# Three of seven products by 512-column passes in a fused encoder layer on one Trainium2 core

## The chip, the cores and the metric

The kernel runs on one core of one Trainium2 chip. The metric is the device time of one execution in microseconds. Engines are named as in the profile: PE (TensorE), with its weight loads PEld apart, DVE (VectorE), ACT (ScalarE), POOL (GpSimd) and SP (SyncE), which issues most of the transfers.

## The reference

One encoder layer on x of 512 positions by 1024 channels, all in float32: a half-step SwiGLU, a mixer (a Fourier group beside grouped-query attention), and a second half-step SwiGLU, each behind an RMSNorm, with a last RMSNorm at the end. The change lies in the two SwiGLUs alone; their inner width is 2752.

```python
def swiglu(h, w_gate, w_up, w_down):
    return (jax.nn.silu(h @ w_gate) * (h @ w_up)) @ w_down

x = x + 0.5 * swiglu(rms_norm(x, ffn1_norm), ffn1_w_gate, ffn1_w_up, ffn1_w_down)
...
x = x + 0.5 * swiglu(rms_norm(x, ffn2_norm), ffn2_w_gate, ffn2_w_up, ffn2_w_down)
return rms_norm(x, final_norm)
```

## The kernel before

Activations lie turned, channels on the partitions and the 512 positions along the row. Every float32 operand is held as a high part, rounded to float32r, and a low part, the rest; a product is three: high by high, high by low, low by high.

**The FFN.** The inner width is cut into 21 blocks of 128 columns (j = 0 to 20) and a tail "t". `ffn` runs once for each SwiGLU. The first four blocks (three in the second FFN) and the tail go through plain gate and up products (`gate`, tile gu). All later ones, 17 and 18, go through `seven`: gate and up of a block together are a two-by-two matrix product over halves of the channels and halves of the positions, made in seven half-sized products in place of eight. The blocks form four groups; behind each stand its down products (`down`, tile dn), which go on while the next block's weights are prepared.

**The seven products.** For a block j, `prepare` loads gate and up weights (raw_g, raw_u), makes four sums (s1 to s4, in tiles s12 and s34) and splits seven weight operands into high and low parts in slots of 1024 words of the tile ring: a11 and a12 together, s1 and s2 together, s3 and s4 together (`both`: high parts in one slot, low parts in another), and a22 alone (`single`: its high part in a slot's first 512 words and its low part in the last). The seven operands on the activation side, b11, b22, b21 and t1 to t4, are made once per FFN by `operands`, in four steps i of one channel tile each, and lie in the tile rt: 2048 words each, high and low parts side by side in 256 + 256 columns, the n-th beginning at n * 2048 + PART_AT[n].

`multiply` runs one product in KH = 4 k steps. For weights not named in WIDE a step has three passes of 256 columns: high weights by high operand and by low operand into the same 256 columns (L436), and low weights by high operand (L441). For those in WIDE the first two are one pass of 512 columns over the operand's high and low parts (L432), which leaves two half sums in 512 columns of PSUM, and the low weights' pass goes to the first 256; both read and write in a turned order of four-word pieces. Whoever takes the result then adds the halves (`added`, `kept`). `step` gives the order on PE per block: a11 (into bank r), a12 (bank p), a22 of the block before (into that block's r), s1 (bank q), s2 (r), s4 (q), s3 (r). PIECES says behind which of them which part of the next block's preparation is recorded.

**Orders.** In the FFNs the order of PE and SP is the order in which the code records; DVE, ACT and POOL are ordered by a scheduler. `lows` is a subtraction on DVE. `rest_by_dma` makes a low part in another way: ACT writes the negated high part (L159), and a transfer issued by POOL adds the source onto it (L160). In `single` the low part of a22 comes from `lows`; in `operands` the b parts of the later steps i come from `rest_by_dma`, the t parts from `lows`. In the opening of an FFN some gates' weights take `rest_by_dma` too (gates 5 to 7 of the first FFN, gate 3 of the second).

Of the kernel before, what the change touches and what calls it, by code (L numbers as in the profile page):

```python
# [7 lines left out]
F32R = mybir.dt.float32r  # L8
# [5 lines left out]
P = 128  # L14
S = 512
# [11 lines left out]
ROOM = 64  # L27
# [5 lines left out]
GROUPS2 = ((0, "t", 1), range(2, 8), range(8, 14), range(14, 21))  # L33
PLACES = 7
HALF = S // 2
PART_AT = (0, 48, 96, 128, 128, 128, 128)
WIDE = ('a12', 's4')
USES = "a11", "a12", "s1", "s2", "s4", "s3", "a22"
PIECES = (0, 2, 2, 0, 2, 1, 1)
KH = KD // 2  # L40
# [43 lines left out]
def asf(ap):  # L84
    return ap.bitcast(F32)
# [3 lines left out]
def encoder(ctx, tc, A, out):  # L89
# [39 lines left out]
    def lows(lo, src, hi):  # L129
        nc.vector.tensor_tensor(out=lo, in0=src, in1=asf(hi), op=ALU.subtract)  # L130
# [26 lines left out]
    def rest_by_dma(lo, hi, src):  # L157

        nc.scalar.activation(lo, asf(hi), AF.Copy, scale=-1.0)  # L159
        nc.gpsimd.dma_start(out=lo, in_=src, accum_op=ALU.add)  # L160
# [18 lines left out]
    def turned(ap):  # L179
        return ap.rearrange("p (a b c) -> p b a c", b=4, c=4)  # L180
# [103 lines left out]
    def ffn(norm, after, wgu, wd, wdt, groups, opening, closing):  # L284
# [4 lines left out]
        n_ = norm.n  # L289
        n_plain = len(groups[0])  # L290
        with tc.tile_pool(name=f"act{n_}", bufs=1) as ap, tc.tile_pool(name=f"sums{n_}", bufs=2) as sp:
            room(ap, 128)
            acts = ap.tile([P, PLACES * 2 * S + ROOM], F32R, name=f"at{n_}")
            at = acts[:, FRONT + LOWER : FRONT + LOWER + PLACES * 2 * S].rearrange("p (n a b) -> p n a b", a=2, b=S)
            rt = ap.tile([P, 7 * KH * S + PART_AT[-1] + PART_AT[-1] - PART_AT[-2]], F32R, name=f"rt{n_}")
            wt, raws = [], {}
            free, where = list(range(PLACES)), {}

# [33 lines left out]

            begins = [i * KH * S + o for i, o in enumerate(PART_AT)]
            part = {
# [4 lines left out]
            def parts_at(i0, i1, i):  # L339

                step = begins[i0 + 1] - begins[i0] if i1 > i0 + 1 else KH * S
                c = rt[:, begins[i0] : begins[i0] + (i1 - i0) * step].rearrange("p (n r) -> p n r", r=step)
                return (c[:, :, i * S + o * HALF : i * S + (o + 1) * HALF] for o in range(2))

            def operands(rp, i0, i1):
                for i in range(i0, i1):
                    b = sp.tile([P, 4, HALF], F32, tag="raw_g", name=f"b{n_}_{i}")
                    for o, k in ((0, i), (2, i + KH)):
                        nc.vector.scalar_tensor_tensor(
                            out=b[:, o : o + 2].rearrange("p a b -> p (a b)"), in0=x[k],  # L350
                            scalar=gains[:, norm.n, k : k + 1], in1=rp, op0=ALU.mult, op1=ALU.mult,
                        )
                    b12, b11, b22, b21 = (b[:, o] for o in range(4))
                    t = sp.tile([P, 4, HALF], F32, tag=("s12", "s34")[i % 2], bufs=1, name=f"t{n_}_{i}")
                    for o, (p, q) in enumerate(((b12, b11), (b22, t[:, 0]), (b22, b12), (b21, t[:, 1]))):
                        nc.vector.tensor_tensor(out=t[:, o], in0=p, in1=q, op=ALU.subtract)
                    for src, i0, i1 in (b[:, 1:], 0, 3), (t, 3, 7):
                        h, l = parts_at(i0, i1, i)
                        nc.scalar.copy(h, src)
                        if i0 or i < (1 if n_ else 2):  # L360
                            lows(l, src, h)
                        else:
                            rest_by_dma(l, h, src)
# [4 lines left out]
            def take():  # L368

                taken.append((own or shared).pop(0))  # L370
                return taken[-1]
# [6 lines left out]
            def prepare(j):  # L378

                g = sp.tile([P, KD * P], F32, tag="raw_g", name=f"raw_g{n_}_{j}")  # L380
                u = wp.tile([P, KD * P], F32, tag="raw", name=f"raw_u{n_}_{j}")
                for t, c in ((g, 2 * j), (u, 2 * j + 1)):
                    nc.sync.dma_start(out=t.rearrange("p (a b) -> p a b", b=P), in_=wgu[c])
                a11, a12, a21, a22 = g[:, :S], g[:, S:], u[:, :S], u[:, S:]
                s12 = sp.tile([P, 2 * S], F32, tag="s12", bufs=1, name=f"s12_{n_}_{j}")
                s34 = sp.tile([P, 2 * S], F32, tag="s34", bufs=1, name=f"s34_{n_}_{j}")
                w = {}

                def both(names, src):
                    hi, lo = (take() for _ in range(2))  # L390
                    nc.scalar.copy(hi, src)  # L391
                    lows(lo, src, hi)
                    for i, n in enumerate(names):
                        w[n] = tuple(t[:, i * S : (i + 1) * S] for t in (hi, lo))
                    w[max(names, key=USES.index), "slots"] = hi, lo

                def single(n, src):
                    t = take()
                    hi, lo = t[:, :S], t[:, S:]
                    nc.scalar.copy(hi, src)  # L400
                    lows(lo, src, hi)
                    w[n] = hi, lo
                    w[n, "slots"] = (t,)

                def combine(out, a, b, op):
                    nc.vector.tensor_tensor(out=out, in0=a, in1=b, op=op)

                return w, [
                    (both, ("a11", "a12"), g),
                    (combine, s12[:, :S], a21, a22, ALU.add),  # L410
                    (combine, s12[:, S:], s12[:, :S], a11, ALU.subtract),
                    (both, ("s1", "s2"), s12),
                    (single, "a22", a22),
                    (combine, s34[:, :S], a11, a21, ALU.subtract),
                    (combine, s34[:, S:], a12, s12[:, S:], ALU.subtract),
                    (both, ("s3", "s4"), s34),
                ]

            def seven(js, done):

                done = [done]
                banks = {}
                count = iter(range(2, 84 * len(js)))

                def multiply(ps, wn, on, w, first):

                    whi, wlo = w[wn]
                    for i in range(KH):
                        ks, m = slice(i * P, (i + 1) * P), part[on][:, i]
                        start, stop = first and i == 0, i == KH - 1  # L430
                        if wn in WIDE:
                            nc.tensor.matmul(turned(ps), whi[:, ks], turned(m), start=start, stop=False, skip_group_check=True)  # L432
                        else:
                            for o in range(2):
                                for t in parts_of(next(count)):
# [3 lines left out]
                                    )  # L439
                        o, m = (turned(q[:, :HALF]) if wn in WIDE else q[:, :HALF] for q in (ps, m))  # L440
                        nc.tensor.matmul(o, wlo[:, ks], m, start=False, stop=stop, skip_group_check=True)  # L441
                    give(*w.get((wn, "slots"), ()))

                def added(out, ps, other, n):
                    nc.vector.tensor_tensor(out=out, in0=ps[:, :HALF], in1=other, op=ALU.add)
                    if n in WIDE:
                        nc.vector.tensor_tensor(out=out, in0=ps[:, HALF:], in1=out, op=ALU.add)

                def kept(out, ps, wide=False):
                    nc.scalar.copy(out, ps[:, HALF:] if wide else ps[:, :HALF])  # L450
                    if wide:
                        nc.vector.tensor_tensor(out=out, in0=ps[:, :HALF], in1=out, op=ALU.add)
# [4 lines left out]
                def step(j, w, n):  # L457
# [22 lines left out]
                    elif n == 6:  # L480
                        multiply(b["r"], "s3", "t3", w, False)
                        b["u"] = tp.tile([P, S], F32, tag="u", name=f"u{n_}_{j}")
                        u = b["u"][:, :HALF]
                        if "s3" in WIDE:
                            nc.scalar.copy(b["u"], b["r"])
# [5 lines left out]
                    elif n == 9:  # L491
                        multiply(b["r"], "a22", "t4", w, False)
                        u, i = b["u"], place(j)
                        h, l = at[:, i, 0], at[:, i, 1]
                        kept(u[:, HALF:], b["r"], "a22" in WIDE)
                        nc.vector.tensor_tensor(out=u, in0=b["g"], in1=u, op=ALU.mult)
# [4 lines left out]
                for s in range(7 * len(js)):  # L501
                    i, n = divmod(s, 7)
# [77 lines left out]
            for gi, group in enumerate(groups):  # L580
# [4 lines left out]
                else:  # L585
# [8 lines left out]
                    for i, c in enumerate(left):  # L594
                        pss.setdefault(c // 2, []).append(gate(c, by_dma=i in (1,) if n_ else i > 0))
                        if due:
                            j = due.pop(0)
# [176 lines left out]
    with in_order():  # L774
        ffn(n0, n1, A["wgu1"], A["wd1"], A["wdt1"], GROUPS1, opening1, None)
# [667 lines left out]
    with in_order():  # L1443
        ffn(n2, n3, A["wgu2"], A["wd2"], A["wdt2"], GROUPS2, lambda gate, column, row: [[gate(0, {KD - 1: column}), gate(1, {3: row})]], closing)
# [122 lines left out]
```

## Time and profile before

| | |
|---|---|
| runs | 819.93, 821.62 and 1694.37 us; median 821.62 |
| profiled execution | 820.24 us, of it the span 818.1 us |
| granted TensorE clock | 0.998 |
| products of `seven` | 35 blocks: L436 1400 passes, L441 980, L432 280 |

A group's row reads: line, engine, operation, tiles written and read, shapes, count, then busy time in us and mean ns of one, then the engine's idle time ahead of it and what ended it. A matmul's mean includes the drain, which overlaps the next one, so the pace of passes is read from their starts. The time of one product is the distance from its first pass to the next product's first pass. The largest groups are the down products and `seven`:

```profile
L186 PE MATMUL dn<-at,ring 128*128 128x512 f32 x900 | 202.5, 380 | 0.0
L436 PE MATMUL r<-rt,ring 128*128 128x256 f32 x1120 | 196.9, 277 | 0.0
L441 PE MATMUL r<-rt,ring 128*128 128x256 f32 x560 | 154.8, 277 | 0.0
L432 PE MATMUL p<-rt,ring 128*128 128x512 f32 x140 | 49.3, 386 | 0.0
L432 PE MATMUL q<-rt,ring 128*128 128x512 f32 x140 | 48.5, 383 | 0.0
```

### The profile page before, as it was taken

How to read it: one execution, taken by the hardware profiler on the slowest of the kernel's cores; microseconds unless marked ns; L12 is line 12 of the kernel's file. 1: busy time of each engine (PE TensorE's matmuls, PEld its weight loads, DVE VectorE, ACT ScalarE, POOL GpSimd, SP SyncE). 2: the span in 40 equal slices, each digit the busy share in tenths (PEclk: the TensorE clock that was granted, in tenths of full speed). 3: DMA queues.
4: the chain of work that ended last, by engine and by line, in shares of the span. 5: the costliest groups of instructions: out<-in, count | busy, mean ns of one | idle time of the engine just before them, and what ended most of it. 6: DMA issues, size and time to landing. Idle time of an engine off the chain costs nothing.

```text
span 818.1 us, 13082 instructions
## 1 busy us (share of the span) xinstructions
PE 811.6 (99%) x5076; PEld 735.5 (90%) x5076; DVE 659.9 (81%) x1073; ACT 483.9 (59%) x810; POOL 29.3 (4%) x31
## 2 busy tenths in 40 slices
PE   9999999999999999999999999999999999999997
PEld 7888999899989998889998888899988999899987
DVE  7898997489956957799998578999955997489674
ACT  7773664257523735689999448556632674257462
POOL 0110000000000000221000001100000000000001
PEclk9999999999999999999999999999999999999999
DMA  7765322424142313342101235543243332333222
GB/s 258 174 145 175 129 93 72 129 104 143 58 143 82 99 58 117 129 148 66 66 26 53 77 104 135 123 164 120 91 123 111 130 102 66 133 104 97 69 78 103
DMA packets 31565, 89.92 MB, mean 110 GB/s; under 512 B 3728, under 2 KB 9232, under 8 KB 31504
## 3 DMA queue, kind: packets, MB, share of 16 engines
q1 hardware_dynamic: 27776, 82.61, 31.2%
q0 software_dynamic: 3008, 5.51, 3.7%
q10 hardware_dynamic: 720, 0.98, 0.3%
q8 instruction: 39, 0.64, 0.3%
q14 instruction: 22, 0.18, 0.1%
HBM read 84.24 MB, written 2.10 MB: 106 GB/s over the span
## 4 chain that ended last, share of the span: by engine, by line
PE 97%; ACT 1%; DVE 0%; DMA 0%; issue 0%; POOL 0%; POOLq 0%; DVEq 0%; ACTq 0%
PE dn L186 25%; PE r L436 16%; PE mix L186 8%; PE r L441 8%; PE gu L186 8%; PE q L436 4%; PE q L441 4%; PE p L432 4%; PE q L432 4%; PE gu L740 3%; PE p L441 2%; PE mix L1234 2%; PE mix L1200 2%; PE mix L1038 1%; PE mix L1039 1%; PE mix L1040 1%
## 5 line engine op out<-in xcount | busy, mean ns | idle before, releaser
L186 PE MATMUL dn<-at,ring 128*128 128x512 f32 x900 | 202.5, 380 | 0.0
L436 PE MATMUL r<-rt,ring 128*128 128x256 f32 x1120 | 196.9, 277 | 0.0
L186 PEld LDWEIGHTS dn<-at,ring 128*128 128x128 f32 x900 | 168.0, 188 | 28.3
L436 PEld LDWEIGHTS r<-rt,ring 128*128 128x128 f32 x1120 | 169.9, 188 | 3.0
L441 PE MATMUL r<-rt,ring 128*128 128x256 f32 x560 | 154.8, 277 | 0.0
L441 PEld LDWEIGHTS r<-rt,ring 128*128 128x128 f32 x560 | 105.1, 188 | 0.0
L391 ACT CAST ring<-s 128x1024 fp32r<-128x1024 f32 x70 | 73.6, 1051 | 36.9 <-PE r L436 27.5
L575 DVE SCALAR_TENSOR_TENSOR gx<-dn,gx 128x512 f32<-128x512 f32 x61 | 41.8, 688 | 65.6 <-PE dn L186 65.6
L130 DVE TENSOR_TENSOR ring<-s,ring 128x1024 fp32r<-128x1024 f32 x70 | 85.3, 1219 | 7.5 <-ACT ring L391 7.1
L172 ACT CAST ring<-raw_dn 128x768 fp32r<-128x768 f32 (+3 forms) x58 | 45.3, 784 | 71.7 <-PE dn L186 60.4
L441 PE MATMUL q<-rt,ring 128*128 128x256 f32 x280 | 76.9, 275 | 0.0
L130 DVE TENSOR_TENSOR ring<-raw_dn,ring 128x768 fp32r<-128x768 f32 (+3 forms) x58 | 51.5, 891 | 5.8 <-PE r L436 4.4
L441 PEld LDWEIGHTS q<-rt,ring 128*128 128x128 f32 x280 | 52.6, 188 | 0.0
L130 DVE TENSOR_TENSOR ring<-raw_g,ring 128x1024 fp32r<-128x1024 f32 x35 | 42.7, 1219 | 11.0 <-PE p L432 9.6
L436 PE MATMUL q<-rt,ring 128*128 128x256 f32 x280 | 49.5, 276 | 0.0
L432 PE MATMUL p<-rt,ring 128*128 128x512 f32 x140 | 49.3, 386 | 0.0
L186 PE MATMUL gu<-ring 128*128 128x512 f32 x216 | 48.9, 381 | 0.0
L432 PE MATMUL q<-rt,ring 128*128 128x512 f32 x140 | 48.5, 383 | 0.0
L186 PEld LDWEIGHTS gu<-ring 128*128 128x128 f32 x216 | 40.4, 188 | 6.9
L450 ACT COPY u<-r 128x256 f32<-128x256 f32 x70 | 26.1, 373 | 34.6 <-PE r L441 34.3
L391 ACT CAST ring<-raw_g 128x1024 fp32r<-128x1024 f32 x35 | 36.8, 1050 | 14.2 <-DMA raw_g<-in_wgu 10.8
L436 PEld LDWEIGHTS q<-rt,ring 128*128 128x128 f32 x280 | 42.2, 188 | 0.2
(275 smaller groups left out, 1543.2 us busy)
## 6 DMA issues: line engine op xcount, KB each, us to landing
raw_g<-in_wgu SPq DMA_DIRECT2D x35, 512.0 KB, 3.7
raw_u<-in_wgu SPq DMA_DIRECT2D x35, 512.0 KB, 4.4
raw_dn<-in_wd SPq DMA_DIRECT2D x40, 384.0 KB, 3.2
raw_gu<-in_wgu SPq DMA_DIRECT2D x12, 512.0 KB, 3.5
raw_o<-in_wo SPq DMA_DIRECT2D x8, 512.0 KB, 3.4
raw_dn<-in_wd SPq DMA_DIRECT2D x8, 448.0 KB, 3.4
raw_wq<-in_wins SPq DMA_DIRECT2D x4, 512.0 KB, 3.5
raw_f<-in_winf SPq DMA_DIRECT2D x4, 512.0 KB, 3.5
```

Of the source, the lines that this page charges most:

```text
L130: nc.vector.tensor_tensor(out=lo, in0=src, in1=asf(hi), op=ALU.subtract)
L172: nc.scalar.copy(hi[:, :n, :], raw[:, :n, :])
L186: nc.tensor.matmul(ps, a, b, start=first and b is mhi and a is whi, stop=last and a is wlo)
L391: nc.scalar.copy(hi, src)
L432: nc.tensor.matmul(turned(ps), whi[:, ks], turned(m), start=start, stop=False, skip_group_check=True)
L436: nc.tensor.matmul(ps[:, t], whi[:, ks], m[:, o * HALF :][:, t], start=start and o == 0, stop=False, skip_group_check=True,)
L441: nc.tensor.matmul(o, wlo[:, ks], m, start=False, stop=stop, skip_group_check=True)
L450: nc.scalar.copy(out, ps[:, HALF:] if wide else ps[:, :HALF])
L575: nc.vector.scalar_tensor_tensor(out=x[d][:, t], in0=ps[:, t], scalar=0.5, in1=x[d][:, t], op0=ALU.mult, op1=ALU.add)
L740: nc.tensor.matmul(turned(pss[c]), w[:, k % 2, c], turned(m[k]), start=k == 0 and m is hh and w is hi, stop=k == KD - 1 and w is lo,)
L1200: nc.tensor.transpose(pts[n][:, c * P : (c + 1) * P], prob[t, b, c][:, kc * P : (kc + 1) * P], ident)
L1234: nc.tensor.matmul(turned(outs[t, b]), w, turned(p), start=kc == 0 and i == 0, stop=kc == 3 and i == 1)
```

## The change

Four things change together. a22 joins WIDE: its four k steps go by a pass of 512 and one of 256, and `kept` adds its halves on DVE (L452). The places of the operands in rt move: b22, b21 and t4 to 48 words past a multiple of 64, the others stay at a multiple of 64. Since places of unequal steps can't be written as one pattern, `operands` casts in four pieces (b11; b22 and b21; t1 to t3; t4) where there were two; b11's low part always comes by transfer, that of b22 and b21 by transfer but for the first step, those of t1 to t4 by DVE. The low part of a22 comes by transfer from the weights in memory. The last edit, the end of the count, has no effect, as no index reaches it.

```diff
-PART_AT = (0, 48, 96, 128, 128, 128, 128)
-WIDE = ('a12', 's4')
+PART_AT = (0, 48, 48, 64, 64, 64, 112)
+WIDE = ('a12', 's4', 'a22')
...
-            rt = ap.tile([P, 7 * KH * S + PART_AT[-1] + PART_AT[-1] - PART_AT[-2]], F32R, name=f"rt{n_}")
+            rt = ap.tile([P, 7 * KH * S + -(-PART_AT[-1] // ROOM) * ROOM], F32R, name=f"rt{n_}")
...
-                    for src, i0, i1 in (b[:, 1:], 0, 3), (t, 3, 7):
+                    for src, i0, i1 in (b[:, 1:2], 0, 1), (b[:, 2:], 1, 3), (t[:, :3], 3, 6), (t[:, 3:], 6, 7):
                         h, l = parts_at(i0, i1, i)
                         nc.scalar.copy(h, src)
-                        if i0 or i < (1 if n_ else 2):
+                        if i0 > 2 or (i0 and i == 0):
                             lows(l, src, h)
                         else:
                             rest_by_dma(l, h, src)
...
                     nc.scalar.copy(hi, src)
-                    lows(lo, src, hi)
+                    rest_by_dma(lo.rearrange("p (a b) -> p a b", b=P), hi.rearrange("p (a b) -> p a b", b=P), wgu[2 * j + 1][:, KH:])
...
-                count = iter(range(2, 84 * len(js)))
+                count = iter(range(2, 2 + 84 * len(js)))
```

The tile rt keeps its size, so nothing else moves in SBUF. The order of SP is the same. On PE only the passes of a22 differ; in the first FFN, block 5, between a12 of block 5 (bank p_5) and s1 (bank q_5), one k step of a22 of block 4 (bank r_4) before:

```order
L441 MATMUL p_5_827<-rt_129,ring 128x4x16x4
L436 MATMUL r_4_712<-rt_129,ring 128x256 x2
L441 MATMUL r_4_712<-rt_129,ring 128x256
L436 MATMUL q_5_861<-rt_129,ring 128x256 x2
L441 MATMUL q_5_861<-rt_129,ring 128x256
```

and after:

```order
L441 MATMUL p_5_850<-rt_129,ring 128x4x16x4
L432 MATMUL r_4_734<-rt_129,ring 128x4x32x4
L441 MATMUL r_4_734<-rt_129,ring 128x4x16x4
L436 MATMUL q_5_881<-rt_129,ring 128x256 x2
L441 MATMUL q_5_881<-rt_129,ring 128x256
```

Two passes of 256 became one turned pass of 512 (4 x 32 x 4), and s1 now follows a turned pass. On ACT, the same place, from the cast of block 6's a22 (raw_u_6) on, before:

```order
L400 CAST ring<-raw_u_6_807 128x512
L450 COPY p_5_862<-q_5_861 128x256
L497 CAST at_128<-u_4_801 128x512
L450 COPY u_5_888<-r_5_812 128x256
L391 CAST ring<-s_0_6_811 128x1024
```

and after:

```order
L400 CAST ring<-raw_u_6_830 128x512
L450 COPY p_5_882<-q_5_881 128x256
L159 ACTIVATE ring<-ring 128x512
L450 COPY u_5_908<-r_5_835 128x256
L497 CAST at_128<-u_4_824 128x512
L391 CAST ring<-s_0_6_834 128x1024
```

The negation (L159) for a22's low part stands behind the copy of s1's result (p_5 from q_5), and ahead of the cast of s3 and s4 (s_0_6). On POOL, in the opening of the first FFN, the difference from the norm (r_91) on; at_128 and ring x2 are the low parts of gates 5, 6 and 7, b_i the operands of step i:

```order
 L258 TENSOR_TENSOR r_91<-ms_92,mhalf 128x4
 L160 DMA at_128<-in_wgu 128x1024
+L160 DMA rt_129<-b_0_379 128x256
+L160 DMA rt_129<-b_1_434 128x256
+L160 DMA rt_129<-b_1_434 128x2x256
 L160 DMA ring<-in_wgu 128x1024 x2
-L160 DMA rt_129<-b_2_480 128x3x256
-L160 DMA rt_129<-b_3_531 128x3x256
+L160 DMA rt_129<-b_2_491 128x256
+L160 DMA rt_129<-b_2_491 128x2x256
```

Three operand transfers now stand ahead of the last two gates' in POOL's queue.

## The prediction

> **What bounds the kernel now.** I read the page first: the head, the busy line of the engines and the chain that ended last.
>
> ```profile
> span 818.1 us, 13082 instructions
> PE 811.6 (99%) x5076; PEld 735.5 (90%) x5076; DVE 659.9 (81%) x1073; ACT 483.9 (59%) x810; POOL 29.3 (4%) x31
> PE 97%; ACT 1%; DVE 0%; DMA 0%; issue 0%; POOL 0%; POOLq 0%; DVEq 0%; ACTq 0%
> ```
>
> The chain is TensorE from end to end. A busy PE need not be PE at its peak, so next I asked the waits of PE and of its weight loads for what they waited for. Outside the first six microseconds the longest is half a microsecond:
>
> ```profile
> PEld mix L1174 <- DVE near L130: 0.5, 1, 0.5
> ```
>
> So the passes follow one another, and time can come only from fewer or denser passes, and be lost only where a new wait opens. Third, the busy time by stage, for how much room the helpers have (columns: window, its length, PE, PEld, DVE, ACT, POOL, clock, DMA share, GB/s): the opening of the first FFN, and its first group of six column blocks by seven products.
>
> ```profile
> 27.00:54.00 27.00, 27.00 (x125) 23.03 (x124) 26.59 (x48) 22.32 (x31) 5.43 (x5) 1.00 0.76 150
> 74.00:130.00 56.00, 56.00 (x447) 54.23 (x446) 52.55 (x83) 35.67 (x63) 0.00 (x0) 1.00 0.29 97
> ```
>
> VectorE is nearly full in both, ScalarE has a third free in the group and a sixth in the opening. These are the places where a cover can be lost.
>
> **The passes themselves.** The chain in order of time, narrowed to the first FFN's first group, gives the start of each product (start, us, what). A row under p begins a12, the first r row behind it a22, the q L436 row s1, the next r row s2, the q L432 row s4, the r row behind that s3 and then a11.
>
> ```profile
> 102.73 0.22 PE p L432
> ...
> 104.09 0.24 PE r L436 x2
> ...
> 108.18 0.22 PE q L432
> ...
> 109.52 0.23 PE r L436 x2
> ...
> 112.25 0.22 PE p L432
> ...
> 113.61 0.24 PE r L436 x2
> ...
> 117.70 0.22 PE q L432
> ...
> 119.04 0.23 PE r L436 x2
> ...
> 121.77 0.22 PE p L432
> ...
> 123.13 0.24 PE r L436 x2
> ...
> 124.50 0.23 PE q L436 x2
> ...
> 125.86 0.23 PE r L436 x2
> ...
> 127.22 0.22 PE q L432
> ...
> 128.56 0.23 PE r L436 x2
> ```
>
> By differences: a12 (512 + 256 columns) takes 1.36 in all three blocks, s4 (the same passes) 1.34 in all three, a22 (three passes of 256) 1.37, s1 and s2 (three of 256) 1.36. From 119.04 to 121.77 s3 and a11 take 2.73: of three-pass products the one behind a wide product costs 1.37, the others 1.36. So width by itself buys almost nothing here (a12 against s2: 0.00); what separates a12 from s4 is where the operand lies. In the built program a12's weights and operand begin 48 and 0 words past a multiple of 64, s4's 48 and 16. After the change all three wide products stand 32 words from their weights, as s4 does.
>
> *Sum on PE, per block:* a12 1.36 to 1.34, a22 1.37 to 1.34, and s1, now behind a wide product, 1.36 to 1.37: 0.02 + 0.03 - 0.01 = 0.04. The rows' hundredths leave 0.03 to 0.06. There are 35 blocks (each product in four k steps), so 1.0 to 2.1 us; I take 0.045, since the three repeats agree: 1.6 us. b11, t1, t2 and t3 stay at the same remainder (32 of 64), so the four products that read them keep their time.
>
> The Trainium skill, "TensorE: Matmul & The Clock Gate", section Back-to-back issue gap, puts an isolated warm pass at N/2.4 + 2.5 ns, so one pass of 512 saves 2.5 ns against two of 256, wherever operands lie; by it the 140 pairs that a22 gives up would save 140 x 2.5 ns = 0.35 us, an estimate. The trace agrees for a12 and not for s4.
>
> **What the other engines get.** The rows for the kinds of instruction involved:
>
> ```profile
> L130 DVE TENSOR_TENSOR ring<-raw_u,ring 128x512 fp32r<-128x512 f32 x35 | 23.9, 682 | 0.0
> L447 DVE TENSOR_TENSOR g<-p,g 128x256 f32<-128x256 f32 x35 | 14.6, 417 | 0.1
> L400 ACT CAST ring<-raw_u 128x512 fp32r<-128x512 f32 x35 | 21.8, 624 | 11.5 <-PE q L436 10.3 <-ACT u L450 0.9 <-DMA raw_u<-in_wgu 0.3
> L450 ACT COPY p<-q 128x256 f32<-128x256 f32 x35 | 12.8, 364 | 0.0
> L359 ACT CAST rt<-t 128x1024 fp32r<-128x1024 f32 x8 | 8.2, 1044 | 0.2
> L159 ACT ACTIVATE rt<-rt 128x768 fp32r<-128x768 f32 x5 | 4.1, 840 | 0.1
> ```
>
> Per block, DVE loses one subtraction of 512 (0.68) and gains one addition of 256 from PSUM (L452, priced as L447: 0.42): 0.26 less of about 9. ACT gains one L159 of 512; rows give 0.62 (a cast of 512) to 0.84 (L159 of 768), I take 0.63: six in the 56 us window are 3.8, from 35.7 to 39.5. Neither is on the path as long as weights stay ahead. How far ahead they are, from the timeline around one block: DVE's subtraction for a11 and the one for s3 and s4, and PE's start of a11.
>
> ```profile
> 115.78 1.22 DVE L130 TENSOR_TENSOR ring<-raw_g,ring 128x1024 fp32r<-128x1024 f32 x1
> 121.13 1.21 DVE L130 TENSOR_TENSOR ring<-s,ring 128x1024 fp32r<-128x1024 f32 x1
> 120.25 0.39 PE L436 MATMUL r<-rt,ring 128*128 128x256 f32 x2
> ```
>
> a11's are ready at 117.00, 3.3 ahead; s4's at 122.34, 4.9 before 127.22. Even if ACT's whole extra 0.63 delays them, over 2.6 remain. Cost zero; without that cover it would be up to 0.63 a block, 22 us in all.
>
> *The correction of a22 by transfer.* Behind the cast stands ACT's copy of p, which waits for the product s1, then L159, then POOL's DMA:
>
> ```profile
> 106.79 0.63 ACT L400 CAST ring<-raw_u 128x512 fp32r<-128x512 f32 x1 [0.91 <-PE q L436]
> 107.32 0.36 ACT L450 COPY p<-q 128x256 f32<-128x256 f32 x1
> 122.97 0.40 PE L436 MATMUL r<-rt,ring 128*128 128x256 f32 x2
> DMA to landing us min/median/max: 4.9/5.6/6.5
> L160 POOL DMA_DIRECT2D rt<-b x5: 1250/1287/1829, 45.4 to 513.9; - x5
> ```
>
> L159 would end at 107.68 + 0.63 = 108.3; a22 of that block starts at 122.97, 14.7 later. POOL needs 1.3 to 1.8 for an issue and has one every 9.5 us, the landing takes 4.9 to 6.5 (for 384 to 512 KB; these are 256), counted from the issue. About 9 us of cover remain. Nothing else stands in POOL's queue in the groups.
>
> *Ends of the two last groups.* There a22's result is needed within its own group, through ACT's copy, now DVE's addition, the product, the cast and the subtraction:
>
> ```profile
> 303.15 0.37 ACT L450 COPY u<-r 128x256 f32<-128x256 f32 x1 [3.47 <-PE r L441]
> 304.93 0.69 DVE L130 TENSOR_TENSOR at<-u,at 128x512 fp32r<-128x512 f32 x1 [0.69 <-ACT at L497]
> 302.95 7.42 PE L186 MATMUL dn<-at,ring 128*128 128x512 f32 x33
> ```
>
> The low part is there at 305.62; PE wants it behind 15 + 1 passes of 0.22, at 306.5. The 0.42 plus a hand-over of some 0.04 leaves 0.4. Cost zero; with a weight subtraction of about 1 us in DVE's way, 0.6, twice: 1.2.
>
> *Openings.* Operands are cast in four pieces instead of two and b11 always goes by transfer. In the first FFN, between the first gate by transfer and the last gate's negation, ACT had two casts of 768 and two of 1024 for them, 3.7 us by the rows above (768 as L159's 0.84). Now it has five of 256, three of 512, two of 768 and negations of 256, 256 and 512: 7 x 0.36 + 4 x 0.62 + 2 x 0.84 = 6.7. Of the extra 3.0 some goes into its idle time, 27.00 - 22.32 = 4.7 us in that window; I let 1 us of it show (0 to 3).
>
> ```profile
> 42.03 0.86 POOL L160 DMA_DIRECT2D ring<-in_wgu  x1 [5.18 <-ACT ring L159]
> 44.09 10.72 PE L186 MATMUL gu<-ring 128*128 128x512 f32 x48
> ```
>
> The transfer lands at 47.6 to 48.5; PE reaches that gate after 24 passes of 0.22, at 49.4, and its low weights two passes later, at 49.8: 1.3 to 2.2 of cover against 1. I take zero, up to 1.7. The second FFN's single gate by transfer gets only 0.2 more ahead of it. DVE is relieved by a subtraction of 768 (it keeps 512 of one piece).
>
> *Total:* the profiled execution took 820.24 us (span 818.1 and 2.1 around it). 820.24 - 1.6 = **818.6 us**. The median of 821.62 is of three runs with one far outlier; the other two, 819.93 and 821.62, lie 0.0 to 0.2% from the profiled one.
>
> **Rivals.** *Width only:* if the 1.34 of s4 is not the placement but, say, its joining a bank already begun, a12 stays and a22 becomes a second a12 (1.36), s1 pays 0.01: nothing, **820.2**. Against it: a22 joins a begun bank too. *Opening transfers late (slower):* POOL now issues three operand transfers ahead of the two gates' ones in the first FFN; if each gate's correction waits for one more landing of 5.6, the last gate misses its 49.8 by 5.6 + 1 - 2.2 to 1.3, about 5: **823.6**. It decides once that landing comes after 49.8. For it: DMA is at 0.76 in that window; against: the operands' transfers are small and issued some us earlier. *a22's correction late (slower):* it decides when issue and landing together take over 14.7 us; at 16 each block stalls 1.3, 46 us, **about 864**. The Trainium skill has a rule for this, "SBUF — State Buffer", box on the "DVE blocks DMA" trap: while DVE runs a two-port operation GpSimd can't write descriptors, and its transfers starve. Against it here: with DVE busy 26.59 of 27.00 us transfers still landed within 6.5. The same page's section Who interferes with whom counts two-input operations out, and that is what DVE runs in these rows.
>
> **How the numbers follow.** Forecast 0.71, width only 0.10, opening transfers 0.11, a22's correction 0.05, the rest 0.03. The forecast's own range is 816.9 (2.1 saved and 1.2 for spread between runs) to 821 (nothing saved but small stalls); with the opening rival's part it is 816.5 to 823.0. Faster or slower by over 2% (16 us; about what a measurement of this kernel can tell from no change): faster 0.02, as no term reaches it; slower 0.06, the correction of a22 and a little unnamed; within 0.92.
>
> **What would show it.** In the new chain, p, the r rows by L432 and q should all last 1.34 per product and s1 1.37; the period of a block falls from 9.52 to 9.48. DVE's share falls by a per cent, ACT's rises by three. A row "PEld r <- DMA ring" at L441 would show the a22 rival, "PEld gu <- DMA" near 49 us the opening. Wrong at the root would be any r L432 product at 1.36, or three-pass products that change.

## The result and the profile after

| | before | after |
|---|---|---|
| executions, same sitting | 819.93 to 824.0 (12 of 13; one more took 1694.37) | 818.77 to 819.7 (13) |
| median, us | 821.69 | 819.1 |
| ratio | | 0.9969, interval 0.996 to 0.9979 |
| profiled execution, span | 820.24, 818.1 | 819.07, 817.3 |

The execution of 1694.37 us was disturbed and stands outside the ratio. The time fell by 0.3%, far inside 2%. The head of the page of after, the busy line and the chain that ended last:

```profile
span 817.3 us, 13006 instructions
PE 809.9 (99%) x4936; PEld 729.0 (89%) x4936; DVE 652.0 (80%) x1080; ACT 503.5 (62%) x870; POOL 67.7 (8%) x75
PE 96%; DMA 1%; DVE 1%; ACT 1%; issue 0%; POOL 0%; POOLq 0%; DVEq 0%; ACTq 0%
```

PE has 140 passes fewer and is still the chain. The two windows of the prediction, same columns:

```profile
27.00:54.00 27.00, 27.00 (x124) 23.06 (x123) 26.88 (x51) 25.31 (x44) 10.14 (x10) 1.00 0.94 211
74.00:130.00 56.00, 56.00 (x427) 53.57 (x426) 50.97 (x83) 38.44 (x68) 5.17 (x6) 1.00 0.48 130
```

In the group DVE gave up 1.58 us for its six blocks (0.26 each), ACT took 2.8 more. In the opening ACT took 3.0 more, and the 16 DMA engines went from 0.76 to 0.94. The chain in order of time, for three blocks of the first group (start, us, what):

```profile
102.23 0.22 PE p L432
...
103.56 0.22 PE r L432
...
104.90 0.23 PE q L436 x2
...
106.27 0.23 PE r L436 x2
...
107.63 0.22 PE q L432
...
108.96 0.23 PE r L436 x2
...
111.70 0.22 PE p L432
...
113.03 0.27 PE r L432
...
114.43 0.24 PE q L436 x2
...
115.84 0.23 PE r L436 x2
...
117.26 0.22 PE q L432
...
118.59 0.24 PE r L436 x2
...
121.33 0.22 PE p L432
```

By differences the first block has a12 1.33, a22 1.34, s1 1.37, s2 1.36, s4 1.33, s3 and a11 together 2.74, and the period to the next p is 9.47. The second block shows something that was not expected. The first pass of a22 starts late (0.27 in place of 0.22), a22 takes 1.40, and the two narrow products behind it take 1.41 and 1.42; s4 is at 1.33 and s3 with a11 at 2.74 again, and the period is 9.63. The waits of PE's weight loads name what held it, and one more:

```profile
PEld dn L186 <- DVE ring L130: 1.0, 2, 0.8
PEld dn L186 <- DVE at L130: 0.4, 1, 0.4
PEld r L432 <- ACT u L489: 0.4, 2, 0.2
```

The last row is a22 waiting at bank r until ACT has copied s3's result out of it. The first is a down product waiting for its weights' low part, and it is not in the profile of before. It stands at 155 us, behind the first group of the first FFN. The waits of DVE from 145 to 160, in before:

```profile
DVE s L406 <- DMA raw_u<-in_wgu: 0.9, 1, 0.9
```

and the same in after, with DVE's timeline there:

```profile
DVE s L406 <- DMA raw_u<-in_wgu: 1.9, 1, 1.9
```

```profile
153.79 0.68 DVE L406 TENSOR_TENSOR s<-raw_g,raw_u 128x512 f32<-128x512 f32 x1
154.40 0.95 DVE L130 TENSOR_TENSOR ring<-raw_dn,ring 128x768 fp32r<-128x768 f32 x1
```

In DVE's queue the subtraction for the down weights stands behind two sums that need raw_u, and raw_u's transfer ended later than in before; so the down product stood still until 155.35.

All stretches of PE, worked out from the starts of its passes (us; "seven" is from the first pass of a group's seven products to the end of its last a22, with the few down passes between them; "down" is what follows up to the next group; the middle is from the end of the first FFN's last a22 to the second FFN's first product):

| | head | seven 1 | down 1 | seven 2 | down 2 | seven 3 | middle | seven 4 | down 4 | seven 5 | down 5 | seven 6 | end |
|---|---|---|---|---|---|---|---|---|---|---|---|---|---|
| before | 73.22 | 61.09 | 27.72 | 61.09 | 27.72 | 51.32 | 234.80 | 61.09 | 27.72 | 61.09 | 27.72 | 61.09 | 35.91 |
| after | 72.86 | 60.95 | 28.41 | 60.78 | 27.72 | 50.82 | 235.19 | 60.78 | 27.72 | 60.78 | 27.72 | 61.00 | 35.91 |

The six stretches of seven products lose 1.66 us. The 245 products in them, each from its first pass to the next product's first pass, sum to 333.64 us before and 332.00 after. Down 1 gives back 0.69. Head and middle move by 0.4 either way. Two executions of one program differ as much: the head is 73.22 here and 72.76 in the repetition of before, the middle 235.19 here and 234.84 in that of after.

### The profile page after: what moved, and what is told of

Same layout as the page of the kernel before. It is cut to its first block, busy times and chain, and to the rows that moved or that the text cites. A ratio compares the mean times of both kernels' runs of the same rounds, so it can differ in the third digit from the quotient of the medians.

```text
span 817.3 us, 13006 instructions
## 1 busy us (share of the span) xinstructions
PE 809.9 (99%) x4936; PEld 729.0 (89%) x4936; DVE 652.0 (80%) x1080; ACT 503.5 (62%) x870; POOL 67.7 (8%) x75
## 3 DMA queue, kind: packets, MB, share of 16 engines
HBM read 93.41 MB, written 2.10 MB: 117 GB/s over the span
## 4 chain that ended last, share of the span: by engine, by line
PE 96%; DMA 1%; DVE 1%; ACT 1%; issue 0%; POOL 0%; POOLq 0%; DVEq 0%; ACTq 0%
PE dn L186 24%; PE r L436 12%; PE mix L186 8%; PE r L441 8%; PE gu L186 8%; PE q L436 4%; PE q L441 4%; PE r L432 4%; PE p L432 4%; PE q L432 4%; PE gu L740 3%; PE p L441 2%; PE mix L1234 2%; PE mix L1200 2%; PE mix L1038 1%; PE mix L1039 1%
## 5 line engine op out<-in xcount | busy, mean ns | idle before, releaser
L441 PE MATMUL r<-rt,ring 128*128 128x256 f32 x560 | 154.3, 276 | 0.0
L436 PE MATMUL r<-rt,ring 128*128 128x256 f32 x840 | 147.1, 276 | 0.0
L436 PEld LDWEIGHTS r<-rt,ring 128*128 128x128 f32 x840 | 127.0, 188 | 1.6
L441 PEld LDWEIGHTS r<-rt,ring 128*128 128x128 f32 x560 | 105.1, 188 | 0.2
L160 POOL DMA_DIRECT2D ring<-in_wgu x38 | 32.9, 867 | 470.9 <-ACT u L450 358.0
L441 PEld LDWEIGHTS q<-rt,ring 128*128 128x128 f32 x280 | 52.6, 188 | 0.0
L436 PE MATMUL q<-rt,ring 128*128 128x256 f32 x280 | 49.8, 277 | 0.0
L432 PE MATMUL r<-rt,ring 128*128 128x512 f32 x140 | 48.7, 384 | 0.0
```

Of the source, the lines that this page charges most:

```text
L436: nc.tensor.matmul(ps[:, t], whi[:, ks], m[:, o * HALF :][:, t], start=start and o == 0, stop=False, skip_group_check=True,)
```

## Experiments

Two theories stood at first. By one (A), the shorter passes are all there is; by the other (B), the helpers' relief also ends the longer executions that before has and after has not (its 13 spread over 0.9 us, those of before over 4). Where a sum is given, it is that of the products as above; the ratio is to before in the same sitting.

**The kernel before, once more.** No edit.

> The kernel before once more, against itself. The products' own time fell by 1.64 us from the one profile to the other, the medians by 2.6, and the kernel before spreads over 819.9 to 824.0 where the changed one keeps to 818.8 to 819.7. Passes alone (theory A): ratio 1.000, and what lies over 820 is stretches in which the passes themselves run slower, seen as 0.35 in place of 0.34 per k step. Helpers (theory B): what lies over 820 is PE waiting for DVE or ACT in some executions, and the profile of a slow one names them.

Measured: 820.12 (819.64 to 822.87), ratio 0.9999 (0.9987 to 1.0011); sum 333.83. So a comparison of this kind tells 0.2% apart, and executions above 821 (here three of eleven) belong to the kernel before.

**The old places.** The kernel before, with its operands and casts, but a22 is wide and corrected by transfer.

```diff
-WIDE = ('a12', 's4')
+WIDE = ('a12', 's4', 'a22')
...
-                    lows(lo, src, hi)
+                    rest_by_dma(lo.rearrange("p (a b) -> p a b", b=P), hi.rearrange("p (a b) -> p a b", b=P), wgu[2 * j + 1][:, KH:])
```

> The changed kernel with the operands' old places and old casts; a22 stays wide and by transfer. Theory A: a12 goes back to 1.36, a22 (operand 16 words before its weights, modulo 64) is near a12's 1.36, s1 keeps 1.37: nothing saved by passes, 820.2 to 821. If width alone saved, a22 would be at 1.34 and the time at 819.5. Theory B (the transfer relieves DVE and makes the times even): spread under 1 us as in the changed kernel, and about 820.2.

Measured: 820.79, ratio 1.0001 (0.9992 to 1.001). The chain in order of time:

```profile
102.45 0.22 PE p L432
...
103.81 0.23 PE r L432
...
105.17 0.24 PE q L436 x2
```

a12 and a22 at 1.36 each; the sum is 333.62, 0.02 from before. Width alone buys nothing, and none of the shorter median comes with it. Of the estimate of 0.35 us by the Trainium skill, "TensorE: Matmul & The Clock Gate", section Back-to-back issue gap (140 fewer passes at 2.5 ns), this run shows none.

**The old width.** Places, casts and transfer as in after, a22 in three passes of 256.

```diff
-WIDE = ('a12', 's4', 'a22')
+WIDE = ('a12', 's4')
```

> The changed kernel with a22 in three passes of 256; places, casts and transfer stay. Theory A: a12 at 1.334, a22 at 1.37, s1 at 1.36: 0.027 x 35 = 0.9 us under the kernel before by passes, 0.7 over the changed one, 819.8. Theory B: times as even as the changed kernel's. The rival that placement does nothing: a12 at 1.36, and 820.2 or more.

Measured: 822.38, ratio 1.0026 (1.0014 to 1.0037), 2.6 us over the expectation. The chain:

```profile
102.27 0.22 PE p L432
...
103.60 0.24 PE r L436 x2
...
105.02 0.23 PE q L436 x2
```

a12 has its 1.33, but a22 takes 1.42: the place that suits a wide pass costs a narrow one 0.05 us a product. The sum is 335.50, 1.86 above before. So a place has no price of its own, only one for a form of pass, and the two edits belong together.

**No transfer for a22's correction.** `single` subtracts on DVE again.

```diff
-                    rest_by_dma(lo.rearrange("p (a b) -> p a b", b=P), hi.rearrange("p (a b) -> p a b", b=P), wgu[2 * j + 1][:, KH:])
+                    lows(lo, src, hi)
```

> The changed kernel with a22's low part by DVE's subtraction again; places, casts and width stay. Theory A: the same products as the changed kernel, 819.1, DVE busier by 0.68 x 35 = 24 us. Theory B: DVE, now with the extra addition and no relief, makes PE wait: times of 820 to 823 with a spread of 2 us or more, and waits of PE or its weight loads for DVE in the blocks.

Measured: 823.09, ratio 1.0035 (1.0021 to 1.0049). By their medians the products are those of after; the waits of the weight loads are not:

```profile
PEld dn L186 <- DVE at L130: 2.4, 3, 1.0
PEld dn L186 <- DVE ring L130: 2.2, 2, 1.2
```

With DVE at 53.0 of 56 us in the group (50.97 in after) the covers are gone. The transfer saves nothing by itself; it pays for the wide a22's addition.

**The transfer alone.** before, with a22's low part by transfer and nothing else.

> The kernel before with nothing but a22's low part by transfer. Passes unchanged, products at 1.36, 1.37, 1.34 as before. Theory A: same, 820.2 to 820.5, ratio 1.000. Theory B (DVE's relief of 0.68 per block ends the long executions): fastest runs at 819.7 as before, but a spread under 1.5 us and a ratio of 0.999.

Measured: 821.74 (820.69 to 824.08), ratio 1.0012 (1.0 to 1.0024). DVE is relieved (50.31 of 56 us), but the spread stays: the theory of the helpers falls in this form. There is a new wait, `PE r L436 <- ACT u L489`. ACT's timeline in the wait at 272 us:

```profile
270.26 0.84 ACT L172 CAST ring<-raw_dn 128x768 fp32r<-128x768 f32 x1 [2.15 <-DMA raw_dn<-in_wd]
...
271.53 1.03 ACT L391 CAST ring<-s 128x1024 fp32r<-128x1024 f32 x1
272.47 0.36 ACT L489 COPY u<-r 128x256 f32<-128x256 f32 x1
```

The copy that frees bank r stands last, behind a cast that waited 2.15 us for the down weights' transfer; a22 started 0.49 us late. Here ACT's queue carries a stall of a transfer over to PE.

**The changed kernel, once more.** No edit.

> The changed kernel once more, beside the others on one chip. Theory A (passes alone, 1.6 us less, and up to 1 us of new waits): 818.8 to 819.4, ratio 0.998 to 0.999 against the kernel before at 820.3. Theory B (the kernel before also loses some us in a part of its executions, and the change ends that): again a spread under 1 us, ratio 0.997 to 0.998, with the kernel before spreading to 822 and more.

Measured: 817.9 (817.71 to 818.32), ratio 0.9965 (0.9952 to 0.9978); sum 331.57. Its down 1 is 28.18, so the stall there comes again, with 0.46 us. The ratio lies below what either theory expected; the spread, 0.6 us, is as B had it.

**Other places.** The changed kernel with operands elsewhere, first PART_AT = (4, 4, 16, 68, 72, 76, 84), then (20, 24, 40, 80, 92, 104, 120).

> The changed kernel with each operand at another place. Distance from operand to weights in words modulo 64 (the changed kernel has 32 for the wide ones, 48 for the others): wide s4 52, a12 0, a22 4; narrow a11 52, s1 52, s2 56, s3 60. Theory A (the distance sets the pace, per form): the down products stand at 52 with 0.220 per 512, so s4 at 52 lasts 1.32 to 1.33; 0 and 4 were never seen, 1.33 to 1.40. The narrow ones leave 1.36 to 1.37, up or down by 0.01 to 0.06, as a22 in three passes did at 32 (1.42). Theory C (only 32 is good for wide and only 48 for narrow): all seven worse. If distance were nothing, all would stay.

> The same at distances s4 8, a12 24, a22 40 (wide), a11 4, s1 0, s2 12, s3 24 (narrow). Theory A: a smooth or periodic dependence, 24 and 40 alike as neighbours of 32, 1.33 to 1.36 wide; narrow 1.32 to 1.42, none known. Theory C: all seven worse than in the changed kernel.

Measured, two executions each: 830.43, ratio 1.0116 (1.0097 to 1.0135), and 830.16, ratio 1.0113 (1.0094 to 1.0132). All seven products became longer, as theory C had it; the guess for s4 at 52, 1.32 to 1.33, missed (1.367). With all runs together, the median of a product by the distance between the start of its weights and that of its operand, in words modulo 64 (us; wide is four times 512 and 256, narrow twelve times 256):

| distance | 0 | 4 | 8 | 12 | 16 | 24 | 32 | 40 | 48 | 52 | 56 | 60 |
|---|---|---|---|---|---|---|---|---|---|---|---|---|
| wide | 1.354 | 1.376 | 1.352 | | 1.361 | 1.383 | 1.334 | 1.354 | 1.366 | 1.367 | | |
| narrow | 1.426 | 1.425 | | 1.418 | 1.413 | 1.429 | 1.421 | | 1.360 | 1.404 to 1.439 | 1.418 | 1.409 |

The entry for narrow at 16 is from the next run but one. 32 is the best of the wide, and 48 the only good one of the narrow. The table has two limits. The weights begin 48 words past a multiple of 64 in every run, so it can't tell the distance from the operand's own place; no run moved the weights. And the product ahead counts too: in the second of these runs a11 and a12 of each group's first block, behind down products, take 1.395 and 1.356, in the later blocks 1.425 and 1.383.

**The place of a12 alone.** Casts and transfer of after, a22 narrow at its old distance of 48.

```diff
-PART_AT = (0, 48, 48, 64, 64, 64, 112)
-WIDE = ('a12', 's4', 'a22')
+PART_AT = (0, 48, 48, 64, 64, 64, 64)
+WIDE = ('a12', 's4')
```

> The new casts and the transfer of the changed kernel, but the operand of a12 alone moved (to 32 words from its weights); a22 stays narrow with its operand at 48 words as before, and two products are wide as before. By the reading of the runs so far (a place has a price that depends on the form of the pass: 32 words are best for the 512-column passes and bad for the 256-column ones, 48 the other way) a12 takes 1.334 us in place of 1.361, a22 1.36 to 1.37 as before and not the 1.42 of the run with a narrow a22 at 32 words, and the sum of the products is 0.93 us below before: 819.4 where the kernel before gives 820.3. The rival, that the new casts or the new layout as a whole and not the place made a22 slow in that run, gives a22 near 1.42 again and a sum 0.8 us above before. As to the spread: if the added work of DVE in the wide a22 has a part in the executions above 821, this kernel, with less of it than either, spreads by under 1.5 us.

Measured: 821.01 (819.77 to 823.02), ratio 0.9982 (0.9966 to 0.9998). The chain:

```profile
102.50 0.22 PE p L432
...
103.84 0.23 PE r L436 x2
...
105.21 0.23 PE q L436 x2
```

a12 1.34 and a22 1.37: the reading holds, and the rival (casts or layout as a whole) falls. The sum is 333.21 and not 332.7: at two places PE waits for ACT's copies, 0.45 us at 272 us (a22's, as with the transfer alone) and 0.22 at 554 us (s3's), and these two products take 0.11 to 0.12 more each; the stall of before near 286 us (last section), some 0.4 in all, is not in it. The executions spread over 3.2 us, not 1.5, so the expectation on the spread missed.

**Narrow operands at 16.** PART_AT = (32, 48, 48, 96, 96, 96, 112).

> The changed kernel with the operands of a11, s1, s2 and s3, all of 256-column passes, at 16 words from their weights (64 words on: modulo 64 the distance is 16) in place of 48. If what counts is how far the two are from 0 and 32, on either side, 16 is as good as 48: those four products keep 1.360 to 1.372 us and the time is that of the changed kernel, 817.9 to 819.1. If 48 is good for a reason of its own, as the other seven distances tried suggest, each of the four takes 1.40 to 1.44, and 35 blocks of four give 6 to 9 us more, 824 to 828.

Measured: 826.86, ratio 1.0057 (1.0038 to 1.0075). Each of the four narrow products takes 1.413: 16 is no mirror of 48. a12 and s4, unmoved at 32, take 1.348 and 1.345 here in place of 1.334, behind the slower narrow products.

**A fourth wide product.** s3 as well, at a distance of 32.

```diff
-PART_AT = (0, 48, 48, 64, 64, 64, 112)
-WIDE = ('a12', 's4', 'a22')
+PART_AT = (0, 48, 48, 64, 64, 112, 112)
+WIDE = ('a12', 's4', 's3', 'a22')
...
-                    for src, i0, i1 in (b[:, 1:2], 0, 1), (b[:, 2:], 1, 3), (t[:, :3], 3, 6), (t[:, 3:], 6, 7):
+                    for src, i0, i1 in (b[:, 1:2], 0, 1), (b[:, 2:], 1, 3), (t[:, :2], 3, 5), (t[:, 2:], 5, 7):
```

> The changed kernel with s3 by 512-column passes as well, its operand at 32 words from the weights; DVE takes one more addition of 128x256 in each block (0.42 us of 9.48) and ACT copies 128x512 in place of 128x256. By the sum of passes s3 takes 1.334 in place of 1.372 and the product behind it at most 0.012 more: 0.9 to 1.3 us saved in 35 blocks, 816.6 to 818.2 against 817.9 to 819.1. The rival: DVE, busy for 51.0 us of the 56 of the first steady stretch and for 53.8 of 57 in the second projection's opening, now lacks 0.42 us more in each block, ACT's longer copy holds bank r against a22, and the waits of PE for DVE's corrections and ACT's copies grow past the saving: 819 to 822.

Measured: 822.41 (819.71 to 824.53), ratio 0.9998 (0.998 to 1.0016): the rival. The products did become shorter (s3 1.333, a11 behind it 1.372, sum 331.14). But the seven's stretches are longer than after's, as the first row of the waits of the weight loads says, and DVE's timeline at the first of the places:

```profile
PEld dn L186 <- DVE at L130: 2.1, 5, 0.4
```

```profile
131.89 0.42 DVE L486 TENSOR_TENSOR u<-u 128x256 f32<-128x256 f32 x1
132.22 0.69 DVE L130 TENSOR_TENSOR at<-u,at 128x512 fp32r<-128x512 f32 x1
```

At a group's end the first down product's last inner block needs the low part made at 132.22, and the added sum (L486) stands right ahead of it. Four of six group ends lose 0.27 us each. The profiled execution is the shortest of the twelve; what the median has above it, 2.7 us, stands in no trace.

**The same, with a22 sooner.** At the group ends the last a22 goes ahead of that inner block.

```diff
-                    for _ in range(len(group) - (last and d < 2)):
+                    for _ in range(len(group) - (last and d < 2) - (gi > 0 and d == 0)):
```

> The kernel with four wide products, and at the ends of the groups the last a22 one inner block sooner: the first down product runs all but its last inner block, then a22, then that block. In the run with four wide products the products came out 0.43 us below the changed kernel's, but at four of the six group ends the down product's last inner block stood still for the low part of its operand (0.37 to 0.39 us for a pass of 0.22, and 0.33 for the next), since DVE's added sum for s3 is queued right ahead of it: 1.1 us. If that is what ate the saving, the four stalls go (every pass of that down product at 0.22), the products keep 1.333 to 1.334 and 1.360 to 1.372, and the time is 1.1 us below that run and 0.4 to 0.9 below the changed kernel: 817.0 to 818.7, a ratio to before of 0.995 to 0.9965. The rival, that DVE is simply short of time with one more addition, lets the stalls return at other places (a22's own bank, or the down weights), and the ratio stays at 0.998 to 1.000.

Measured: 820.52 (818.56 to 821.3), ratio 0.9982 (0.997 to 0.9995). The four stalls are gone, and others stand elsewhere: the first row is of PE's waits, the second of DVE's from 600 to 622 us.

```profile
PE dn L186 <- DVE ring L130: 1.7, 1, 1.7
```

```profile
DVE s L406 <- DMA raw_u<-in_wgu: 3.2, 1, 3.2
```

The first is the wait of after at 155 us once more, now behind a group of the second FFN, since DVE waited 3.2 us for raw_u. So the named stalls were the order's fault, and others came in their place. That the helpers have no time left for a fourth sum is not shown: the largest new stall stands behind a transfer that landed 6.2 us after its issue. None of the runs has a lower ratio to before than the changed kernel as it is.

## Why the prediction was right

*The passes.* a12 and a22 at 1.34, s1 at 1.37, the others unchanged but behind a stall: as worked out, and the sum of 1.6 us met 1.64 (2.07 in the repetition, which has fewer stalls). That width alone does nothing is shown by the run with the old places (sum 0.02 below before), and that the place alone shortens a12 by the run with a12's place; a22 needs both. "Width only" is out. (s4's operand, b22, stood 48 words past a multiple of 64 before as well; only b21 and t4 moved in this respect.) The prediction reads the effect as one of the distance between operand and weights. The runs bear out its numbers, but as the weights never moved, the operand's own place would do as well.

*What the prediction had only half.* It read the distance of 32 as good for the wide products and left the narrow a22 out of it. The run with the old width shows that the same move would have cost a22 0.05 us a block had it stayed narrow.

*Helpers in the group.* DVE's 0.26 a block is met. For ACT 39.5 was predicted and 38.44 came: the six negations took the 3.8 us assumed, and one other instruction fewer lies in the window (68 against 63 + 6). No weights of the seven products came late. The transfer as DVE's cover, put at no cost, is confirmed from both sides: without it the kernel is at 1.0035, alone it is at 1.0012.

*a22's correction by transfer.* The transfers of the weights that POOL issues, with the time to landing:

```profile
L160 POOL DMA_DIRECT2D ring<-in_wgu x38: 858/860/927, 35.6 to 759.7; - x38
...
DMA to landing us min/median/max: 3.7/4.5/7.2
```

In the group shown, the issue for the a22 at 122.5 us stands at 108.54, 14.0 ahead, and the longest landing takes 7.2; nobody waited for one. An issue takes 0.86 and not the 1.3 to 1.8 assumed. The rival at 864 did not come. The rule of the Trainium skill, "SBUF — State Buffer", box on the "DVE blocks DMA" trap, was not put to the test: it speaks of two-port operations, and all of DVE's operations in the opening's window, 26.88 of 27.00 us, have two inputs.

*Group ends and openings.* The covers of 0.4 at the ends of the two last groups held: the end stretch is 35.91 in both kernels, and the one wait for a low part of `at` in after stands at 535 us, in the second FFN's opening. In the opening no gate waited for a transfer, ACT's 3.0 us came as predicted, and they cost nothing. "Opening transfers late" did not come. (Its own price, 823.6, lies above the 823.0 to which the range was stretched for it.)

*The term that was missing.* The sum had no term for the weights of the down products. Behind the first group raw_u lands late, DVE waits for it, and the down weights' correction is queued behind: 0.69 us in one execution, 0.46 in the other. It is larger than the whole distance from the predicted 818.6 to 819.1; head, middle and the time around the span, which vary from one execution to the next, make up the rest. The 9.2 MB that after reads more (93.41 in place of 84.24) don't explain it: without the transfer the reading is that of before, and down 1 is 28.78; with the transfer alone it is 93.41, and down 1 is 27.72 as in before. The DMA queues from 148 to 153 us, while this raw_u is on its way (queue, packets, MB, share of the 16 engines), in before:

```profile
q1 hardware_dynamic: 364, 1.34, 83.5%
```

and in after:

```profile
q1 hardware_dynamic: 306, 1.09, 67.7%
q8 instruction: 1, 0.02, 2.1%
```

In no run does POOL's queue move anything then. What after has is one packet that the profile calls instruction. It is there in all seven profiles in which this raw_u lands 4.4 to 5.3 us after its issue, and in none of the seven in which it lands after 3.6 to 3.9. That the packet holds raw_u up is likely by this, but no run moved it, and why it falls there in some kernels was not followed up. The late raw_u of the last experiment has no such packet beside it and stays open.

*The medians.* From lowest to lowest the gain is 1.2 us, and 1.8 in the repetition, on both sides of the 1.64 of the products; from median to median it is 2.6 and 2.9, because before's executions reach upwards and after's do not. That 818.6 came so near to the median is in part luck: it was counted from an execution at the lower end of before's, and from before's median the same 1.6 us give 820.1. The transfer alone, the place of a12 alone and the wide a22 at the old places all keep a spread of 1.9 to 3.4 us. Where executions differ can be seen by laying their passes side by side. Before and its repetition differ at the first gates (0.4), at 531 us (down products in the second FFN's opening, 0.14) and at 543 and 573 us (0.2 together). The transfer alone differs from before at the first gates, at 272 us (a22 behind ACT's copy of s3's result), at 535 to 537 and at 554 (s3 behind ACT's copy of s2's). Behind the wait at 272 stood a transfer, as shown; for the others it was not followed up. Why the changed kernel's executions don't reach upwards stays open: the two profiles of before are of executions of 820.24 and 820.04, and none is of a long one.

## What to carry to other kernels

Before placing operands, measure each form of pass at each place, in the order in which the products will run; a place that shortens one form lengthened another here by more than the gain. Where PE is full, cost a change by the starts of passes, and then look through every helper's queue for an instruction that waits for a transfer: whatever stands behind it inherits the wait, and this is where the small loss of this change and the largest of the last attempt lay. The losses of the fourth wide product lay behind an added sum instead. List the transfers that have under 2 us of cover, also those that the change doesn't touch: one of them cost 0.69 us here. And before blaming added traffic for a late transfer, look whether it is late without the traffic too.

## What the hardware showed beyond expectation

The pace of passes depends on where the operand lies, and differently for each form: 1.334 to 1.383 us for a product of wide passes, 1.360 to 1.439 for one of narrow passes, over the places tried. Whether its own place counts or its distance from the weights, and by which mechanism, stays open.

A narrow pass has two paces, 113.3 ns and about 117.7 (1.413 us for a product). The second is that of the distance of 16, and it appears at the good one too, for some time behind a stall; at the other distances a pass takes 117 to 120 ns on average. In after, a22's late pass at 113.03 is followed by s1 and s2 at 1.41 and 1.42: 0.06 of waiting and 0.1 behind it. In before it lasts longer. The chain of waits in the last group of its first FFN shows s4's first pass 0.11 us late, and then s3 with a11, and a22, s1 and s2 behind them:

```profile
285.81 0.33 PE q L432
...
287.27 0.24 PE r L436 x2
...
290.10 0.22 PE p L432
...
291.45 0.24 PE r L436 x2
...
295.69 0.22 PE q L432
```

s3 and a11 take 2.83 in place of 2.73, and a22, s1 and s2 together 4.24 in place of 4.10, although two wide products lie between, and the pace stays so to the group's end at 298.44. A stall of 0.11 us costs about 0.3 more by what runs behind it; what ends the slower pace was not found.
